# Rewriting the front of a hybrid transformer block: transposed q and k projections, both heads per scan, an LRU interleaved with attention, and an instruction order from a list schedule

## The chip, the cores and the metric

The kernel runs on one core of one Trainium2 chip. The time is the device time of one execution in microseconds (us). The engines are TensorE (PE, with its weight loads as PEld), VectorE (DVE), ScalarE (ACT), GpSimd (POOL) and SyncE (SP, which here only issues DMAs).

## The reference

One transformer block on 1024 tokens of width 1024, in fp32. A hybrid mixer stands in front, a squared-ReLU MLP behind:

```python
h = rms_norm(x, norm1_g)
proj = h @ w_in                                   # 1024 x 2560
q, k, v, xl, gl = split(proj)                     # five times 512 columns
q = rms_norm(q per head of 64, q_norm_g); k = rms_norm(k per head of 64, k_norm_g)
# stick-breaking attention, 8 heads, strictly causal
z = q @ k.T / 8
w = sigmoid(z) * prod over later keys of (1 - sigmoid(z))    # only keys before the query
attn = w @ v
# RG-LRU on 512 channels
u = causal_depthwise_conv(xl, width 4)
r, i = sigmoid(blockdiag(u, w_rg) + b_rg), sigmoid(blockdiag(u, w_ig) + b_ig)
a = exp(-8 * r * softplus(-lam));  hs[t] = a[t] * hs[t-1] + sqrt(1 - a[t]**2) * i[t] * u[t]
lru = hs * gelu(gl)
x = x + concat([attn, lru]) @ w_out
x = x + square(relu(rms_norm(x, norm2_g) @ w_up)) @ w_down
```

## The kernel before

**Arithmetic.** Nearly every fp32 operand of a product is split into a high part (rounded to the fp32r type) and a low part (the rest), and a product is three matmuls: low by high, high by low, high by high (`mm3`, lines 62 to 65). ACT makes the high part with a copy, DVE or POOL the low part with a subtraction (`lo_part`, line 60).

**Stages.** The front computes everything up to the mixer's output, which it writes channel by channel to `mix_d` in DRAM. Behind it stand the output projection (tiles `po`, fed by `wr_o`, the loads of `w_out`, and `mr`, the loads of `mix_d`) and the MLP with its own ring of loads and a fixed order of its own.

**The front** begins with x: 128-token tiles are loaded, transposed on PE (`ptx`), multiplied by the norm's gain and split into `hTh` and `hTl` (channels on partitions, 1024 tokens). The rows' 1/rms goes in later: `rstd1` multiplies what is projected. Head pairs are called p (0 to 3), each 128 columns of q, k and v.

- `in_proj(p, ..., tp)` projects q, k and v of one pair for 256 tokens, with tokens on partitions: per 128 tokens 24 matmuls of 384 columns into `pd`. DVE squares and sums q and k per head, `rsqrt_mean` finds 1/sqrt by three Newton steps on DVE (lines 84 to 89), DVE multiplies by it, POOL by the gains; then both are split and transposed on PE (`pq`, `pk`, `pl`) into `qT`, `kH`, `kL`. v stays with tokens on partitions (`vv`). In `qT` and `kH` the 128 rows hold the high and the low part of one head of 64, so that one matmul of 128 rows gives two of the three products and a second of 64 rows, with `kL`, the third.
- `attention(p, h, c, ...)` works on one head and two row blocks of 128 queries, r = 2c and 2c+1, over keys in pieces of up to 512. PE makes `z` (lines 405 and 406, and 408 for the mask on the diagonal block), ACT the two sigmoids (lines 410 and 411), DVE the product over later keys by a scan (line 415), POOL `w` times it (line 416). PE transposes w (`pw`, line 426), ACT and DVE split it (`wth`, `wtl`), PE multiplies with v (`av`, line 435), and DVE stores the head's rows through `ob`.
- The LRU's recurrence (`lru_tile`, lines 341 to 366) runs for all four blocks of 128 channels once the first pair is projected: projection `pxl`, convolution, two gates (`pg`, full fp32 matmuls), `Tanh`, a reciprocal on DVE (line 358), `Sqrt`, the scan. The result goes to `lru_d` in DRAM. `gate(c, ch)` later projects `pgl`, computes the gelu by a sigmoid, and multiplies.

**What sets the order.** `ORDER` lists attention units (A p h c), projections (I p tp), weight loads (O, W) and gates (G c ch); Tile's scheduler then moves instructions of neighbouring units past each other where its own model finds it useful, DMA issues on SP's queue among them.

Of the kernel before, what the change touches and what calls it, by code (L numbers as in the profile page):

```python
# [28 lines left out]
NG = 4  # L29
NW = 11  # L30

ORDER = (
# [3 lines left out]
).split()  # L38
EPS = 1e-6
NEG = -1e30  # L40
# [3 lines left out]
def kernel(ctx, tc, x, norm1_g, w_in, conv_w, conv_b, w_rg, b_rg, w_ig, b_ig,  # L44
# [13 lines left out]

# [7 lines left out]

    const = pool(ctx, "const")
    small = pool(ctx, "small", bufs=6)
    dram = pool(ctx, "dram", space=DRAM)
    ps_d = pool(ctx, "ps_d", bufs=2, space=PSUM)  # L70
# [8 lines left out]

    def rsqrt_mean(ssq, n, cols):  # L80
        v = small.tile([P, 8], F32, tag="rs_v", name="rs_v")[:, :cols]
        y = small.tile([P, 8], F32, tag="rs_y", name="rs_y")[:, :cols]
        m = small.tile([P, 8], F32, tag="rs_m", name="rs_m")[:, :cols]
# [9 lines left out]
    def transpose_pair(name, rows, gain, pools, dst_h, dst_l, col):  # L93
        for b in range(KC // 2):
            pt = bank(pools[b % len(pools)], [2, 2, P], f"pt{name}_{b}")
            for j in range(2):
                kc = 2 * b + j
                for i in range(2):
                    nc.tensor.transpose(pt[:, j, i, :], rows[i][:, kc * P:(kc + 1) * P], ident)
            for j in range(2):  # L100
                kc = 2 * b + j
                src = pt[:, j].rearrange("p i t -> p (i t)")
                oh = dst_h[:, kc, col:col + 2 * P]
                nc.scalar.mul(oh, src, gain[:, kc:kc + 1])
                nc.vector.scalar_tensor_tensor(dst_l[:, kc, col:col + 2 * P], src, gain[:, kc:kc + 1], oh.bitcast(F32),
                                               op0=ALU.mult, op1=ALU.subtract)

    nc.scalar.preload_act_table_set("sigmoid_and_others")
    ident = const.tile([P, P], F32, name="ident")
    make_identity(nc, ident)  # L110
    identr = const.tile([P, P], F32R, name="identr")
    identb = const.tile([P, P], BF16, name="identb")
    maskb = const.tile([P, P], BF16, name="maskb")

    mix_d = dram.tile([D, S], F32, name="mix_d")
    lru_d = dram.tile([AW, S], F32, name="lru_d")
    rs_d = dram.tile([NT, P], F32, name="rs_d")
    rs_row = rs_d.rearrange("t p -> (t p)").unsqueeze(0)
    rstd1 = const.tile([P, NT], F32, name="rstd1")
    gain1 = const.tile([P, NT], F32, name="gain1")  # L120
    rs2 = const.tile([P, NT], F32, name="rs2")

    left1 = ExitStack()
    hp = pool(left1, "hT")
    hTh = hp.tile([P, KC, S], F32R, name="hTh")
    hTl = hp.tile([P, KC, S], F32R, name="hTl")
    qkvE = pool(left1, "qkvE")
    wp = pool(left1, "wp", bufs=8)
    mp = pool(left1, "misc")


    def load_w(eng, name, src, n, wr=None):
        if wr is None:
            wr = wp.tile([P, 384], F32, tag="wr", name=f"wr_{name}", bufs=4)[:, :n]
        wh = wp.tile([P, 384], F32R, tag="wh", name=f"wh_{name}", bufs=8)[:, :n]
        wl = wp.tile([P, 384], F32R, tag="wl", name=f"wl_{name}", bufs=8)[:, :n]
        nc.sync.dma_start(wr if len(src.shape) == 2 else wr.rearrange("p (a b) -> p a b", a=src.shape[1]), src)
        nc.scalar.copy(wh, wr)
        lo_part(eng, wl, wr, wh)
        return wh, wl  # L140

    def load_pair(p, engs, raws=None):
        return [load_w(engs[kc % len(engs)], f"p{p}_{kc}",
                       w_in[kc * P:(kc + 1) * P, 0:3 * AW].rearrange("p (a b) -> p a b", a=3)[:, :, P * p:P * (p + 1)], 384,
                       raws[kc] if raws else None)
                for kc in range(KC)]

    XL0 = 3 * AW
    GL0 = XL0 + AW

    def load_cols(name, c0, engs):
        return [load_w(engs[kc % len(engs)], f"{name}_{kc}", w_in[kc * P:(kc + 1) * P, c0:c0 + 256], 256) for kc in range(KC)]

    def proj_cols(ws, j, ch, name):
        pd = bank(ps_d, [512], name)
        for kc in range(KC):
# [829 lines left out]
```

## Time and profile before

| | before |
|---|---|
| time, median of 3 runs | 1190.53 us (1189.09 to 1193.4) |
| span of the profiled execution | 1188.2 us |
| PE busy | 1140.8 us (96%) |
| DVE busy | 934.5 us (79%) |
| ACT busy | 603.7 us (51%) |
| POOL busy | 541.1 us (46%) |
| mean granted clock of PE | 0.983 |
| first matmul of the output projection | 459.0 us |

The profile is one execution. A stretch of the span has its own busy times, so the front (0 to 459 us) is read apart from what follows. The start of a matmul is recorded and its end is modelled: the distance between two starts in a stretch without waits says what one costs, its duration does not.

### The profile page before, as it was taken

To read this page: it belongs to the slowest core of one execution; us is meant where nothing else is said; L and a number is where in the kernel's file an instruction comes from. 1 tells how busy PE (TensorE), PEld (TensorE's weight loads), DVE (VectorE), ACT (ScalarE), POOL (GpSimd) and SP (SyncE) were. 2 spreads that over 40 slices of the span, in tenths; PEclk is the share of its full clock that TensorE was granted. 3 is DMA by queue.
4 is the path that set the end of the run, shared out by engine and by line. 5 is a ranking of instruction groups with operands and counts; after the bars stand their busy time and mean duration, and the time that the engine had idled before them with its cause. 6 is when DMAs were issued, how large, how long until landed. Compare 5 with 4: busy or idle time off the path is not lost.

```text
span 1188.2 us, 16104 instructions
## 1 busy us (share of the span) xinstructions
PE 1140.8 (96%) x5410; PEld 936.0 (79%) x5410; DVE 934.5 (79%) x1458; ACT 603.7 (51%) x1203; POOL 541.1 (46%) x506
## 2 busy tenths in 40 slices
PE   7999999999999968999999999999999999999998
PEld 7876777778888747888878888887887788888787
DVE  7789998899998887224776768998758667889975
ACT  7554665666665663136642584443456127743441
POOL 1357754664446683100244356762303444658331
PEclk9998999999999978999999999999999999999999
DMA  8110010410101284202344323554533333245654
GB/s 268 46 54 36 18 52 28 132 38 7 53 7 35 71 303 133 71 1 81 106 142 124 98 72 98 168 170 152 166 116 116 116 115 98 63 130 162 190 167 158
DMA packets 80787, 123.58 MB, mean 104 GB/s; under 512 B 10256, under 2 KB 28736, under 8 KB 80704
## 3 DMA queue, kind: packets, MB, share of 16 engines
q1 hardware_dynamic: 78400, 118.35, 32.0%
q10 hardware_dynamic: 2304, 4.20, 0.9%
q8 instruction: 43, 0.70, 0.3%
q14 instruction: 40, 0.33, 0.1%
HBM read 107.83 MB, written 14.68 MB: 103 GB/s over the span
## 4 chain that ended last, share of the span: by engine, by line
PE 70%; DVE 16%; issue 5%; DMA 3%; ACT 3%; POOL 2%; SPq 0%; DVEq 0%; ACTq 0%; POOLq 0%
PE p L577 24%; PE pa L577 11%; PE pb L577 5%; PE pc L577 4%; PE po L63 3%; PE po L64 3%; PE po L65 3%; DVE g L415 2%; PE av L435 2%; PE pd L63 2%; PE pd L64 2%; PE pd L65 2%; PE z L406 2%; PE pw L426 2%; POOL r_ea L577 1%
## 5 line engine op out<-in xcount | busy, mean ns | idle before, releaser
L416 POOL TENSOR_TENSOR w<-w,g 128x128 f32<-128x128 f32 (+3 forms) x96 | 101.4, 1064 | 102.7 <-DVE g L415 50.9
L415 DVE TENSOR_TENSOR_SCAN g<-g 128x128 f32<-128x128 f32 (+3 forms) x96 | 112.5, 1184 | 5.0 <-ACT g L410 4.1
L577 POOL TENSOR_TENSOR r_sb<-r_sb,r_sa 128x512 f32<-128x512 f32 x16 | 24.2, 1514 | 183.5 <-DMA r_sb<-in_w_up_dram 158.0
L577 DVE TENSOR_TENSOR U<-p,U 128x512 f32<-128x512 f32 x80 | 55.1, 688 | 63.0 <-PE p L577 62.7
L63 PE MATMUL pd<-wh_p,hTl 128*128 128x384 f32 x256 | 91.7, 359 | 9.5 <-DVE vv L180 4.4
L577 POOL TENSOR_TENSOR U<-U 128x512 f32<-128x512 f32 x48 | 69.4, 1452 | 68.8 <-ACT U L577 44.5
L577 PE MATMUL p<-m1t,st 128*128 128x512 f32 x384 | 91.2, 396 | 2.6 <-DVE U L577 2.6
L577 PE MATMUL p<-m0t,st 128*128 128x512 f32 x384 | 89.6, 391 | 1.3 <-DVE U L577 1.3
L64 PE MATMUL pd<-wl_p,hTh 128*128 128x384 f32 x256 | 90.2, 352 | 0.3 <-DVE wl_p L60 0.3
L577 PEld LDWEIGHTS p<-m1t,st 128*128 128x128 f32 x384 | 73.1, 191 | 19.4 <-issue 3.0
L65 PE MATMUL pd<-wh_p,hTh 128*128 128x384 f32 x256 | 87.9, 343 | 0.0
L577 PEld LDWEIGHTS p<-m0t,st 128*128 128x128 f32 x384 | 71.9, 188 | 17.7 <-ACT sb L577 1.7
L577 PE MATMUL p<-m0b,sb 128*128 128x512 f32 x288 | 68.0, 392 | 0.0
L577 PE MATMUL p<-m1b,sb 128*128 128x512 f32 x288 | 67.3, 391 | 0.0
L577 PEld LDWEIGHTS p<-m1b,sb 128*128 128x128 f32 x288 | 54.1, 188 | 11.8
L577 PEld LDWEIGHTS p<-m0b,sb 128*128 128x128 f32 x288 | 53.8, 188 | 11.5
L577 ACT ACTIVATE U<-U 128x512 f32<-128x512 f32 x96 | 58.9, 630 | 6.1 <-DVE U L577 3.1
L430 ACT CAST wth<-pw 128x512 fp32r<-128x512 f32 (+1 forms) x80 | 42.6, 547 | 37.5 <-PE pw L426 25.5
L410 ACT ACTIVATE g<-z 128x128 f32<-128x128 f32 (+3 forms) x96 | 48.1, 501 | 26.1 <-PE z L408 10.9
L63 PEld LDWEIGHTS pd<-wh_p,hTl 128*128 128x128 f32 x256 | 49.3, 193 | 13.2 <-DVE vv L180 5.3
L60 DVE TENSOR_TENSOR wtl<-pw,wth 128x512 fp32r<-128x512 f32 (+1 forms) x80 | 49.3, 628 | 9.9 <-ACT wth L430 9.5
L426 PE MATMUL pw<-ident,w 128*128 128x128 f32 x288 | 48.2, 285 | 5.4 <-DVE wtl L60 3.0
(302 smaller groups left out, 3218.8 us busy)
## 6 DMA issues: line engine op xcount, KB each, us to landing
wr_p<-in_w_in_dram SPq DMA_DIRECT2D x24, 192.0 KB, 2.7
xt<-in_x_dram SPq DMA_DIRECT2D x8, 512.0 KB, 7.5
wr_o<-in_w_out_dram SPq DMA_DIRECT2D x8, 512.0 KB, 3.8
mr<-mix_d SPq DMA_DIRECT2D x8, 512.0 KB, 6.8
x<-in_x_dram SPq DMA_DIRECT2D x16, 256.0 KB, 6.5
r_a<-in_w_up_dram SPq DMA_DIRECT2D x16, 256.0 KB, 2.7
r_b<-in_w_up_dram SPq DMA_DIRECT2D x16, 256.0 KB
r_sa<-in_w_up_dram SPq DMA_DIRECT2D x16, 256.0 KB
```

Of the source, the lines that this page charges most:

```text
L60: eng.tensor_tensor(lo, src, hi.bitcast(F32), op=ALU.subtract)
L63: nc.tensor.matmul(ps, al, bh, start=start, stop=False)
L64: nc.tensor.matmul(ps, ah, bl, start=False, stop=False)
L65: nc.tensor.matmul(ps, ah, bh, start=False, stop=stop)
L406: nc.tensor.matmul(z, qT[hs, h, qr], kL[hs, k0:k0 + kn], start=False, stop=not diag)
L410: nc.scalar.activation(g[:, :kn], z, AF.Sigmoid, scale=-1.0)
L415: nc.vector.tensor_tensor_scan(gr, gr, gr, g[:, kn:kn + 1], op0=ALU.mult, op1=ALU.bypass)
L416: nc.gpsimd.tensor_tensor(w[:, :kn], w[:, :kn], g[:, 1:kn + 1], op=ALU.mult)
L426: nc.tensor.transpose(pw[:, i * P:(i + 1) * P], wrow[rr][j // 4][:, j % 4 * P:(j % 4 + 1) * P], ident)
L430: nc.scalar.copy(wth[:, :nw], pw[:, :nw])
L435: nc.tensor.matmul(av[:, q0:256], vv[:, 2 * m + jj, h, :], wt[:, 256 * jj:256 * jj + 256 - q0], start=m == 0 and jj == 0 and wt is wtl, st ...
L577: ins = getattr(self.eng, op)(*args, **kw)
```

## The change

Everything of the front is written again; the output projection and the MLP stay, except that `rsqrt_mean` takes one power (-0.5) on POOL in place of the three Newton steps.

A new class `Plan` records each instruction with its engine, an assumed duration, and the tiles that it reads and writes. `record_front` records the units in the sequence of a new `ORDER`: C (constants), X (two token tiles of x), W (weights), R (the row of 1/rms), Q p ch (q and k of a pair for 512 tokens), V (v of two pairs for 512 tokens), L c ch (one LRU block of 128 channels for 512 tokens, with its gelu), A p c (attention of both heads of a pair for two row blocks). `schedule` is a list schedule: at each step the engine that can start earliest takes its ready instruction of the earliest unit; tiles have counted slots. The instructions are then issued in that order, each through `Pinned`, which keeps an engine's instructions in program order.

- **q and k** are projected with channels on partitions (24 matmuls of 512 columns each), so the transposes `pq`, `pk`, `pl` go. The sum of squares per head comes from four full fp32 matmuls with two moving columns (`ones2`), 1/sqrt from a power on POOL; the result is spread over 64 columns by ACT, transposed on PE (`rb`) and multiplied on DVE.
- **v** is projected for two pairs at once, 256 columns.
- **z**: for each row block and piece of keys, three products of 64 rows for each of the two heads, head 0 on partitions 0 to 63 and head 1 on 64 to 127, one after the other in turn, into the two halves of `z` (two banks). One burst holds two row blocks.
- **Sigmoids and scans** take both heads in one instruction: the scan of a diagonal piece runs over both heads' keys, with the constant row `K1` that restarts it at the second head. A piece that continues an earlier one keeps one scan per head.
- **LRU**: `Exp` and `Gelu_apprx_tanh` on ACT in place of the reciprocal and of the sigmoid form of gelu; per block the two `Sqrt`, two `Exp`, two `Gelu` are kept together. Nothing goes through `lru_d`; the row of 1/rms is made on PE in place of the detour through DRAM.

The core of the diff:

```diff
+ORDER = (
+    "C1 C0 X2 Wq0 X3 Wv0 R1 X1 Q01 X0 Wl0 Q00 V00 Wq1 R0 V01 A03 L00 A02 Wl1 L01 Q11 "
+    "Q10 A13 Wq2 L10 A10 L11 Q21 A12 Wv1 Wl2 A00 Q20 A11 V11 Wl3 V10 A22 A23 A01 L20 L21 L30 "
+    "Wq3 L31 A21 Q31 Q30 A20 A33 A32 A30 A31 "
+).split()
...
+    def chain(pd, key, col, ch, name):
...
+                    E.pe.matmul(pd[:], w[:, 1, s], E.hTh[:, kc, m], start=kc == 0, stop=False)
+                    E.pe.matmul(pd[:], w[:, 0, s], E.hTl[:, kc, m], start=False, stop=False)
+                    E.pe.matmul(pd[:], w[:, 0, s], E.hTh[:, kc, m], start=False, stop=kc == KC - 1)
...
+    def qunit(p, ch):
...
+            chain(pd, key, P * w, ch, f"p{'qk'[w]}{p}{ch}")
...
+                for t in range(4):
+                    E.pe.matmul(ps[:, 2 * t:2 * t + 2], sq[:, t * P:(t + 1) * P], E.ones2, start=True, stop=True)
...
+            op("POOL", 1637, lambda w=w: E.gps.tensor_tensor(sm[:, 8 * w:8 * w + 8], sm[:, 8 * w:8 * w + 8], E.mhalf[:, 0:8], op=ALU.pow),
...
+                    E.pe.transpose(rb[:, t * P:(t + 1) * P], sq[:, t * P:(t + 1) * P], E.ident)
...
+            op("DVE", 684, lambda f=f, rb=rb: E.dve.tensor_tensor(f[:], f[:], rb[:], op=ALU.mult), r=[f, rb], w=[f], what=f"nrm{p}{ch}")
...
+    def vunit(pp, ch):
...
+                        E.pe.matmul(pd[:, 0:256], E.hTh[:, kc, s], w[:, 1], start=kc == 0, stop=False)
...
+    def lunit(c, ch):
...
+            op("ACT", 620, lambda T=T: E.act.activation(T[:, 0:512], T[:, 0:512], AF.Sqrt), r=[T], w=[T], set="sqrt", grp=c, what=f"sqrt{nm}")
...
+            op("ACT", 620, lambda y=y: E.act.activation(y[:, 0:512], y[:, 0:512], AF.Gelu_apprx_tanh), r=[y], w=[y], set="gelu", grp=c, what=f"gelu{nm}")
...
+    def aunit(p, c):
...
+                    for n, (a, b) in enumerate(((1, 0), (0, 1), (0, 0))):
+                        for h in range(2):
+                            hs = slice(HD * h, HD * h + HD)
+                            E.pe.matmul(z[:, h, :kn], q[hs, a, cols], k[hs, b, :kn], start=n == 0, stop=n == 2 and not diag)
...
+                    if diag:
+                        gr = G[:, 0:2 * n - 1][:, ::-1]
+                        E.dve.tensor_tensor_scan(gr, gr, E.K1[:, 512 - kn:513 + kn][:, ::-1], 1.0, op0=ALU.mult, op1=ALU.add)
+                        return
...
+    plan = Maker()
+    record_front(plan, E, ORDER)
+    plan.schedule()
+    for o in plan.order:
+        o.fn()
+    front.close()
...
-        nc.vector.tensor_scalar(y.bitcast(I32), v.bitcast(I32), -0.5, float(0x5F3759DF), op0=ALU.mult, op1=ALU.add)
-        for _ in range(3):
-            nc.vector.scalar_tensor_tensor(m, y, -0.5, v, op0=ALU.mult, op1=ALU.mult)
-            nc.vector.tensor_tensor(m, m, y, op=ALU.mult)
-            nc.vector.scalar_tensor_tensor(y, m, 1.5, y, op0=ALU.add, op1=ALU.mult)
+        nc.gpsimd.tensor_tensor(y, v, E.mhalf[:, :cols], op=ALU.pow)
         return y
```

More of the change, by code (lines that the diff above doesn't have):

```diff
@@ new lines, with dve, dve2, act @@
+PTAGS = ("z", "pd", "pw", "av")
+MM = {512: 227, 384: 173, 256: 117, 128: 109}
+KEEP = {"PE": 0, "DVE": -77, "ACT": -95, "POOL": -40, "SP": 0}
+def dve(n):
+    return 210 + 0.93 * n
+def dve2(n):
+    return 230 + 1.45 * n
+def act(n):
+    return 185 + 0.82 * n
+def gps(n):
+    return 350 + 1.95 * n
+class V:
+    def __init__(self, plan, tag, name):
+        self.plan, self.tag, self.name = plan, tag, name
+        self.wr, self.rd, self.real = {}, {}, None
+        self.slot, self.ops, self.allocs = None, {}, []
+        if tag is not None:
+            plan.queue.setdefault(tag, []).append(self)
+    def get(self):
+        if self.real is None:
+            self.real = self.plan.make(self)
+        return self.real
+    def __getitem__(self, k):
+        return self.get()[k]
@@ new lines @@
+    E.pe, E.dve, E.act, E.gps, E.sp = (Pinned(e) for e in (nc.tensor, nc.vector, nc.scalar, nc.gpsimd, nc.sync))
+    E.vec = const.tile([P, 42], F32, name="vec")
+    E.mhalf = const.tile([P, 8], F32, name="mhalf")
+    nc.vector.memset(E.mhalf, -0.5)
+    gain2 = E.vec[:, 32:40]
+    front = ExitStack()
+    fc = pool(front, "fc", side="right")
+    hp = pool(front, "hT", side="right")
+    E.hTh = hp.tile([P, KC, S], F32R, name="hTh")
+    E.hTl = hp.tile([P, KC, S], F32R, name="hTl")
+    for nm, shape in (("rstd1", [NT]), ("var1", [NT]), ("epsv", [NT]), ("gain1", [NT]), ("gcol", [1]), ("t_a", [4]), ("t_b", [4]), ("t_c", [4]),
+                      ("sp_", [4]), ("nsp", [4]), ("ones2", [2]), ("bd", [2, NCT, P]), ("rsb", [S]), ("K1", [1025])):
+        setattr(E, nm, fc.tile([P] + shape, F32, name=nm))
@@ new lines @@
+    E.identb = fc.tile([P, P], BF16, name="identb")
+    E.maskb = fc.tile([P, P], BF16, name="maskb")
+    nc.vector.tensor_copy(E.identb, ident)
+    nc.gpsimd.memset(E.maskb, 0.0)
+    nc.gpsimd.affine_select(out=E.maskb, in_=E.maskb, compare_op=ALU.is_gt, fill=NEG, base=0, pattern=[[-1, P]], channel_multiplier=1)
+    nc.vector.memset(E.ones2, 0.0)
+    for h in range(2):
+        nc.vector.memset(E.ones2[HD * h:HD * h + HD, h:h + 1], 1.0)
+    nc.vector.memset(E.K1, 0.0)
+    nc.vector.memset(E.K1[:, 512:513], 1.0)
@@ new lines, with make @@
+    spools = {t: pool(front, f"f_{t}", space=PSUM if t in PTAGS else None, side=("right" if t in ("w", "wr", "v", "lg", "f", "qk") else None) if t not in PTAGS else None)
+              for t in COUNT}
+    class Maker(Plan):
+        def make(self, v):
+            shape, dt = SHAPE[v.tag]
+            return spools[v.tag].tile([P] + shape, dt, tag=f"{v.tag}{v.slot}", name=v.name)
+    plan = Maker()
[3 more added lines that the diff above has]
+        o.fn()
@@ L90, in rsqrt_mean @@
-        return y
[L93 to L140, printed above, removed]
@@ L494 @@
-    right1.close()
-    left1.close()
+        nc.gpsimd.tensor_tensor(y, v, E.mhalf[:, :cols], op=ALU.pow)
+        return y
     xp1 = pool(ctx, "x1")
```

854 lines of the change are left out of this document (541 added, 313 removed), and 3 rows, old and new, of the table ORDER.

## Prediction

> **What bounds the kernel now.** I read the 40 slices of the page first, which show TensorE (PE) busy nearly everywhere, and then cut the span where the first matmul of the output projection starts, at 459.0 us. The busy times by stretch:
>
> ```profile
> core 0: us, PE busy (x) PEld busy (x) DVE busy (x) ACT busy (x) POOL busy (x), PEclk, DMA share, GB/s
> 0.00:459.00 459.00, 423.45 (x2275) 351.01 (x2275) 407.43 (x773) 277.55 (x630) 242.66 (x316) 0.96 0.24 76
> 459.00:1188.20 729.20, 717.36 (x3136) 584.98 (x3136) 527.07 (x686) 326.15 (x574) 298.48 (x190) 0.99 0.39 122
> ...
> 10.00:420.00 410.00, 392.73 (x2139) 327.36 (x2137) 372.88 (x727) 247.25 (x574) 217.99 (x290) 0.98 0.19 58
> 420.00:459.00 39.00, 25.54 (x118) 19.48 (x118) 31.63 (x37) 23.91 (x45) 22.58 (x18) 0.76 0.62 217
> 459.00:480.00 21.00, 21.00 (x82) 17.06 (x83) 15.81 (x12) 4.64 (x5) 11.47 (x5) 0.88 0.68 224
> ```
>
> The second row is the part behind the front: 729 us, PE busy for 717 of them at a clock of 0.99. The change leaves that part alone but for a few small operations (below), so I carry it over as 729 us. All of the forecast is about the first row. There PE is busy for 423 of 459 us, but VectorE (DVE) for 407 too: two engines are close to full, and the waits of PE say which one holds the other up. The longest waits of PE in the front:
>
> ```profile
> PE av L435 <- DVE wtl L60: 5.8, 2, 5.0
> PE ptx L99 <- DMA xt<-in_x_dram: 4.5, 1, 4.5
> ```
>
> Apart from the first load of x, it is DVE that PE waits for. But a busy PE is not a PE at its peak, since the ends of matmuls are modelled. So I price PE work by the distance between starts, in stretches where nothing waits (columns: start, duration, engine, line, operation, tiles, shape):
>
> ```profile
> 29.26 0.33 PE L63 MATMUL pd<-wh_p,hTl 128*128 128x384 f32 x1
> 29.43 0.33 PE L64 MATMUL pd<-wl_p,hTh 128*128 128x384 f32 x1
> ...
> 93.89 1.02 PE L351 MATMUL pg11r<-u,bd_r 128*128 128x512 f32 x2
> 94.74 1.02 PE L351 MATMUL pg11i<-u,bd_i 128*128 128x512 f32 x2
> ...
> 407.20 0.27 PE L405 MATMUL z<-kH,qT 128*128 128x128 f32 x1
> 407.41 0.32 PE L406 MATMUL z<-kL,qT 64*128 64x128 f32 x1
> 407.66 0.23 PE L408 MATMUL z<-maskb,identb 128*128 128x128 bf16 x1
> 407.70 0.47 PE L64 MATMUL pgl<-hTl,wh_gl 128*128 128x512 f32 x1
> ...
> 408.24 0.40 PE L63 MATMUL pgl<-hTh,wl_gl 128*128 128x512 f32 x1
> 408.48 0.40 PE L64 MATMUL pgl<-hTl,wh_gl 128*128 128x512 f32 x1
> ...
> 411.68 0.28 PE L435 MATMUL av<-wtl,vv 128*128 128x256 f32 x1
> 411.80 0.28 PE L435 MATMUL av<-wth,vv 128*128 128x256 f32 x1
> ...
> 412.56 0.95 PE L426 MATMUL pw<-ident,w 128*128 128x128 f32 x7
> 413.27 0.48 PE L405 MATMUL z<-kH,qT 128*128 128x512 f32 x1
> 413.67 0.50 PE L406 MATMUL z<-kL,qT 64*128 64x512 f32 x1
> 414.10 0.39 PE L405 MATMUL z<-kH,qT 128*128 128x256 f32 x1
> 414.42 0.38 PE L406 MATMUL z<-kL,qT 64*128 64x256 f32 x1
> 414.73 0.23 PE L408 MATMUL z<-maskb,identb 128*128 128x128 bf16 x1
> ```
>
> So a split matmul of 512 columns costs 0.23 us, one of 384 columns 0.17, one of 256 columns 0.12, a transpose 0.10 (seven in 0.71), a full fp32 matmul of 512 columns 0.85 in two passes. The surprise is z: 0.40 and 0.43 at 512 columns, 0.32 and 0.31 at 256, 0.21 and 0.25 at 128. The pair alternates between a form of 128 rows (kH) and one of 64 rows (kL), and every change of form costs some 0.2 us on top of the 0.23.
>
> The front's PE work from that: q, k, v 768 x 0.17 = 132; xl and gl 384 x 0.23 = 88; transposes of x and of the weights w 352 x 0.10 = 36; transposes of q, k and k's low part 160 x 0.10 = 16; av 256 x 0.12 and 64 x 0.10 = 37; gates 16 x 0.85 = 14; z 48 x 0.83 + 16 x 0.74 (384 columns, put between its neighbours) + 16 x 0.63 + 16 x 0.46 + 64 masks x 0.04 = 72. Sum 395 us. Of the 459 us, 64 are therefore lost. Some 20 go in 420 to 459, where PE is busy for 25.5 us at a clock of 0.76, worth 19. Some 5 go at the start (the 4.5 us wait). The other 39 go between 10 and 420: 17 idle (410 less 392.7), 8 by the clock of 0.98, the rest at the seams between groups.
>
> **The change, PE.** q and k transposed: 4 pairs x 2 chunks x 2 x 24 = 384 matmuls x 0.23 = 88; v for two pairs at a time: 384 x 0.12 = 46; against the 132 of before that is nothing. xl and gl stay at 88, the 352 transposes at 36, av at 37, gates at 14. The 160 transposes of q and k go (-16); 64 that carry 1/rms into columns and 8 for the rows' scale come (+7). New are 64 sums of squares, a full fp32 matmul with two moving columns: two passes each. No row shows such a one. Below lies half a transpose a pass (64 x 2 x 0.05 = 6), above the gates' 0.85 each (54). I take a transpose's 0.10 a pass, 13 us, since a transpose too loads 128 columns of weights and streams little.
>
> z is the largest term. It becomes 48 steps of six matmuls of 64 rows, heads 0 and 1 alternating between partitions 0 to 63 and 64 to 127, in 24 bursts, so the form changes twice a burst. If the two heads' matmuls run side by side, a step costs three distances: 24 x 3 x 0.23 + 8 x 3 x (0.17 + 0.12 + 0.10) = 26, with 48 changes x 0.2 and the masks 38. If they run one after the other, 52 + 12 = 64. If going from one half to the other costs as much as the change of form does in the rows above, 144 x 0.43 + 48 x (0.37 + 0.32 + 0.23) + 3 = 109. No row shows two halves at work at once. I take 38: the excess in the rows sits on a change of form, and stays away where the form stays; inside a burst it stays, and the two heads share neither rows of the array nor an output bank.
>
> By the Trainium skill, TensorEngine Tiling (Array Packing), Key Properties, "Different tiles can execute LdWeights and Matmul in parallel", while a change of the tiling mode drains the engine; by that rule z is the 38 that I took. The trace agrees with the second half (0.40 to 0.43 for 0.23); the first half no run here shows yet.
>
> PE's sum after: 88 + 46 + 88 + 36 + 7 + 37 + 14 + 13 + 38 = 367, **28 less** than before; with z's and the sums' other ends, 360 to 479.
>
> **The other engines.** Does one of them take over? The first two rows are DVE's busy time from 0 to 459 on what touches rs_y and sq, the others groups by line and shape (count, busy us, mean ns):
>
> ```profile
> 0.00:459.00 459.00, 58.86 (x220) 0.96 0.24 76
> 0.00:459.00 459.00, 26.26 (x32) 0.96 0.24 76
> ...
> L358 DVE RECIPROCAL ext<-ext 128x512 f32<-128x512 f32 x8 | 26.7, 3341 | 1.1 <-POOL ext L356 1.0
> L60 DVE TENSOR_TENSOR wtl<-pw,wth 128x512 fp32r<-128x512 f32 x48 | 32.5, 684 | 7.7 <-ACT wth L430 7.4
> L348 DVE SCALAR_TENSOR_TENSOR u<-ext,vec,u 128x512 f32<-128x512 f32 x24 | 23.9, 1018 | 2.6 <-ACT u L346 2.4
> L104 ACT ACTIVATE hTh<-ptx,gain 128x256 fp32r<-128x256 f32 x32 | 13.5, 494 | 0.3 <-PE ptx L99 0.3
> L359 ACT ACT_TABLE_LOAD x4 | 5.1, 1283 | 0.1
> ```
>
> DVE loses the Newton steps and the scaling by them (58.9), the squares and their sums (26.3) and the reciprocals (26.7), 112 us. It gains 16 products with the 1/rms tile at 0.68 and 8 joined multiply-adds at 1.02, with small ones some 25. 407 - 112 + 25 = 320 at the most, for other things shrink too: the scan of a diagonal block covers both heads in one instruction. ScalarE (ACT) gains, for q and k, four passes of 512 columns x 16, at about twice the 0.494 of a 256-column one at the most (63 us), and has 16 table loads for 8, +10: 278 + 73 = 351 if nothing of the old q, k path is taken off, and that path goes. GpSimd gains 16 low parts and 16 powers of eight numbers. No row shows a power; between nothing and a reciprocal's 3.3 us each it is 0 to 53, hidden behind other projections either way, and it loses the same kind of low parts elsewhere. All stay under PE's 367. So PE remains the bound, now with no second engine beside it.
>
> **What is lost beside the sum.** Middle: the 17 us of idle wait for a DVE that is 89% full; at 320 of some 425 us it is 75% full, and I leave 4 of the 17. The clock's 8 and the seams stay. Start: what x needs before the first product.
>
> ```profile
> 0.74 0.40 SPq L222 DMA_DIRECT2D xt<-in_x_dram  x1
> ...
> 7.49 0.33 SPq L273 DMA_DIRECT2D vrow<-in_conv_w_dram  x1
> ```
>
> Before, x went out first and the ten small loads later. Now C1's ten small loads stand first on SP's queue, 0.33 us each, 3 us; and the first product needs 512 tokens transposed (16 pieces of 0.494 on ACT) where 256 did (8), 4 us. I take +6, since the weights' casts fill part. End: again attention alone, four units of pair 3, paced by scans; I leave the 20. Handover to the output projection:
>
> ```profile
> 413.25 0.43 SPq L889 DMA_DIRECT2D wr_o<-in_w_out_dram  x1
> ...
> 457.19 0.45 SPq L443 DMA_DIRECT2D mix_d<-ob  x1
> ...
> wr_o<-in_w_out_dram SPq DMA_DIRECT2D x8, 512.0 KB, 3.8
> mr<-mix_d SPq DMA_DIRECT2D x8, 512.0 KB, 6.8
> ```
>
> Before, the first load of w_out was issued 44 us ahead of the last store of attention, past it on SP's queue. Now every instruction of the front is held in its order. If the loads must queue behind the last store, 6.8 us of landing and the casts are open; if they pass, nothing. I take +3, with 0 to 10 as its ends. Behind the front, the four Newton chains on the norm of h become one power on GpSimd, which is idle there (298 of 729 us): nothing either way, and if that cover were gone, a few of at most 3.3 us.
>
> Losses: 64 + 6 - 13 + 3 = 60. The front then ends at 367 + 60 = 427, 32 us earlier; the span is 1188.2 - 32 = 1156. The median of before, 1190.53, lies 2.3 us over its profiled span, so the forecast is **1158.5 us**.
>
> **Rivals.** (1) Better than that: the fixed order fills the middle and half of the end, losses of 30 in place of 60: 1128. For it speaks that only PE is full; against it, that 64 were lost before. (2) The heads run one after the other: +26, 1184. (3) The sums of squares cost the gates' price: +41, 1199. (4) **The order holds PE up:** each q or k chunk goes through eight steps on four engines (square, sum, power, spread, transpose, product, two halves) and PE's next instruction in the fixed order waits at the queue's head, with all matmuls behind it; or the handover pays its 10. Twice the middle's old idle, +17: 1176. (5) **Slower:** going from one half of the array to the other costs what the change of form costs; z is 109, +71: 1229. It decides from 32 us over 288 matmuls, 0.11 us each above the shared price. Only the 0.2 us of the z rows speaks for it. That the change does not do what it says would show as (4), with the old waits in new places.
>
> **How the numbers follow.** Forecast 0.40, (1) 0.20, (2) 0.10, (3) 0.04, (4) 0.17, (5) 0.09. The range reaches from below (1) to (3): 1118 to 1200; outside lie (5) and the far end of (1). What a measurement of this kernel can tell from no change is about 0.5%, 6 us. Faster: forecast, (1), (4), half of (2): 0.82. Same: the rest of (2) and part of (3): 0.08. Slower: 0.10.
>
> **What would show it.** Right: the first output projection near 427 us; two z matmuls of one step starting within 0.1 us of each other; DVE near 300 us in the front; no wait of PE above 5 us between 20 and 400. Wrong: z starts 0.23 or 0.43 apart all along a burst; the sums of squares over 0.3 us apart; PE waiting for GpSimd's power or for ACT behind table loads; or more than 5 us between the last av and the first po. The forecast falls altogether if the part behind the front does not keep its 729 us.

## The result and the profile after

The changed kernel takes 1198.53 us (median of 5 runs, 1197.89 to 1202.43) against 1189.09 of the kernel before (5 runs, 1184.65 to 1193.4): a ratio of 1.0091, 95% interval 1.0066 to 1.0117. It is slower by 0.9%, where 1158.5 us, 2.6% faster, was forecast. The time lies inside the range, on the side that had a chance of 0.10. The profiled execution has a span of 1199.3 us (1188.2 before).

The view of busy times by stretch, for the changed kernel, cut near the first attention product (`z`, at 59.1 us), near the last projection (375.8), and at the last matmul of the output projection (`po`, 571.0):

```profile
core 0: us, PE busy (x) PEld busy (x) DVE busy (x) ACT busy (x) POOL busy (x), PEclk, DMA share, GB/s
0.00:60.00 60.00, 43.43 (x220) 36.05 (x222) 27.38 (x91) 36.52 (x81) 20.59 (x34) 0.91 0.36 115
60.00:376.00 316.00, 309.95 (x1896) 258.79 (x1893) 194.20 (x256) 197.90 (x343) 168.01 (x176) 0.99 0.12 38
376.00:571.00 195.00, 154.06 (x726) 124.66 (x725) 81.88 (x102) 74.40 (x126) 54.68 (x44) 0.80 0.22 75
```

The middle is what the forecast hoped for and more: PE is busy for 310 of 316 us at a clock of 0.99, and DVE for only 194. The third row is where the time went: 195 us in which PE is busy for 154 and gets 0.80 of its clock. The longest waits of PE say by whom it is held there:

```profile
PE av L708 <- DVE wt L708: 25.4, 16, 3.0
PE rb L708 <- ACT sq L708: 9.1, 4, 5.1
...
PE po L697 <- POOL mix0l L694: 4.5, 1, 4.5
PE po L697 <- DVE mix0l L694: 4.2, 1, 4.2
```

`wt` is the tile with the high and low parts of the transposed weights; the product with v (`av`) waits for it. All but two of its 16 waits, and all but 1.5 us of their sum, lie behind 376. Near the end of attention the timeline shows one turn after another (start, duration, engine, line, operation, tiles):

```profile
477.95 1.23 PE L708 MATMUL av<-wt,v 128*128 128x256 f32 x4 [1.40 <-DVE wt L708]
...
478.97 1.05 PE L708 MATMUL pw<-ident,w 128*128 128x128 f32 x4
...
480.06 0.59 ACT L708 CAST wt<-pw 128x512 fp32r<-128x512 f32 x1 [0.48 <-PE pw L708]
480.68 0.69 DVE L708 TENSOR_TENSOR wt<-pw,wt 128x512 fp32r<-128x512 f32 x1 [0.65 <-ACT wt L708]
...
481.43 1.22 PE L708 MATMUL av<-wt,v 128*128 128x256 f32 x4 [1.40 <-DVE wt L708]
...
482.45 0.63 PE L697 MATMUL po<-wo,mix0l 128*128 128x512 f32 x1
```

Four transposes fill the bank `pw`, ACT casts it into `wt`, DVE makes the low part, PE multiplies: 3.48 us from one av to the next, one step after the other (of the 21 such distances behind the last projection the middle one is 3.62). The plan's slots (`COUNT`) hold one `pw` and one `wt`. The kernel before has two of each (`bufs=2` in its lines 72, 428 and 429), and in its timeline the transposes of the next group begin while ACT still casts this one:

```profile
450.71 0.59 ACT L430 CAST wth<-pw 128x512 fp32r<-128x512 f32 x1 [1.39 <-PE pw L426]
...
450.93 0.63 PE L426 MATMUL pw<-ident,w 128*128 128x128 f32 x4
...
451.33 0.69 DVE L60 TENSOR_TENSOR wtl<-pw,wth 128x512 fp32r<-128x512 f32 x1 [1.42 <-ACT wth L430]
451.71 0.59 ACT L430 CAST wth<-pw 128x512 fp32r<-128x512 f32 x1
```

In the changed kernel, as long as projections stand beside, the turn hides behind them; behind the last projection it is all that there is. The tile views of `av`, before and after, from the last projection on (count, duration min/median/max, first and last start):

```profile
L435 PE MATMUL av<-wtl,vv x32: 221/386/583, 416.2 to 456.0; 128*128 128x256 f32 x27, 128*128 128x128 f32 x5
L435 PE MATMUL av<-wth,vv x32: 275/319/416, 416.3 to 456.0; 128*128 128x256 f32 x27, 128*128 128x128 f32 x5
```

```profile
L708 PE MATMUL av<-wt,v x88: 222/415/582, 395.4 to 482.2; 128*128 128x256 f32 x68, 128*128 128x128 f32 x20
```

Before, 64 matmuls of av, 16 groups of four, were left behind the last projection and took 40 us, 2.5 us a group; the first came 0.2 us behind that projection. Now there are 88, 22 groups, the first of them comes 19.5 us behind the last projection, and they take 87 us, 3.9 us a group.

In the timeline of its first burst z shows that the two heads do run side by side: twelve matmuls, six a head, half of them of 384 and half of 512 columns, in 1.43 us up to the mask. One head after the other they would take 2.4 us at the distances of the prediction.

```profile
59.10 1.50 PE L708 MATMUL z<-k,q 64*128 64x384 f32 x12
60.53 0.40 PE L708 MATMUL z<-maskb,identb 128*128 128x128 bf16 x4
```

**The balance.** I price every matmul of the changed kernel by the distances of the prediction, z's changes of form included, and call lost what is left of a stretch:

| stretch | lost, forecast | lost, measured |
|---|---|---|
| start, to 60 us | 5 + 6 = 11 | 25.1 |
| 60 us to the last projection (375.8) | 39 - 13 = 26 | 15.5 |
| end and handover, with the output projection, to the last po (571.0) | 20 + 3, and the 8 that po lost before (94.9 us for 384 x 0.227) = 31 | 76.5 |

The matmuls of the front are those that the prediction counted, so at its prices they come to its 367 again; the part from the last po to the end takes 628.3 us where it took 634.4. So of the 43 us between the forecast span (1156) and the measured one, 14 come at the start, some 45 behind the last projection, and some 16 go the other way: 10 in the middle, 6 in the part behind.

### The profile page after: what moved, and what is told of

It is laid out like the page before. It is cut to its first block, busy times and chain, and to the rows that moved or that the text cites. A ratio compares the mean times of both kernels' runs of the same rounds, so it can differ in the third digit from the quotient of the medians.

```text
span 1199.3 us, 15521 instructions
## 1 busy us (share of the span) xinstructions
PE 1123.8 (94%) x5546; PEld 926.4 (77%) x5546; DVE 792.2 (66%) x1055; ACT 607.1 (51%) x1072; POOL 526.0 (44%) x439
## 4 chain that ended last, share of the span: by engine, by line
PE 71%; DVE 10%; ACT 6%; issue 5%; POOL 5%; DMA 2%; SPq 0%; ACTq 0%; POOLq 0%; DVEq 0%
PE p L859 24%; PE pa L859 9%; PE pq L708 6%; PE pc L859 4%; PE pv L708 4%; PE av L708 3%; PE pgl L708 3%; PE z L708 2%; PE pw L708 2%; PE po L697 2%; PE po L699 2%; PE po L698 2%; PE pb L859 2%; POOL r_ea L859 2%; PE pxl L708 2%
## 5 line engine op out<-in xcount | busy, mean ns | idle before, releaser
L708 POOL TENSOR_TENSOR w<-w,G 128x1024 f32<-128x1024 f32 (+3 forms) x48 | 78.0, 1637 | 57.0 <-ACT w L708 34.1
L708 PE MATMUL pq<-hTh,wq 128*128 128x512 f32 x256 | 89.5, 409 | 1.9 <-ACT rsb L708 1.9
L708 PE MATMUL av<-wt,v 128*128 128x256 f32 (+1 forms) x320 | 60.4, 316 | 26.0 <-DVE wt L708 25.4
L708 DVE TENSOR_TENSOR wt<-pw,wt 128x512 fp32r<-128x512 f32 (+1 forms) x80 | 50.4, 629 | 50.9 <-ACT wt L708 50.2
L708 PEld LDWEIGHTS av<-wt,v 128*128 128x128 f32 x320 | 51.1, 212 | 41.9 <-DVE wt L708 36.2
L859 POOL TENSOR_TENSOR r_sb<-r_sb,r_sa 128x512 f32<-128x512 f32 x16 | 21.5, 1342 | 107.7 <-DMA r_sb<-in_w_up_dram 65.7
L708 ACT CAST wt<-pw 128x512 fp32r<-128x512 f32 (+1 forms) x80 | 43.4, 543 | 42.2 <-PE pw L708 39.8
L859 ACT ACTIVATE U<-U 128x512 f32<-128x512 f32 x96 | 58.9, 629 | 6.4 <-DVE U L859 3.4
L708 DVE TENSOR_TENSOR_SCAN G<-G,K 128x769 f32<-128x769 f32 (+3 forms) x32 | 54.8, 1723 | 9.7 <-ACT G L708 8.8
L708 PEld LDWEIGHTS pq<-hTh,wq 128*128 128x128 f32 x256 | 48.7, 190 | 12.4 <-ACT rsb L708 2.6
L708 ACT ACTIVATE G<-z 128x1024 f32<-128x1024 f32 (+3 forms) x48 | 38.3, 816 | 26.7 <-PE z L708 16.3
```

What stands on the lines that cost most here:

```text
L708: return tc.keep_in_program_order(getattr(self.eng, op)(*args, **kw))
L859: ins = getattr(self.eng, op)(*args, **kw)
```

## The experiments

The theory behind them: the attention that is left alone goes single file through the one `pw` and the one `wt`, and at half the clock. The rivals: the scans on DVE set its pace, as the prediction had it; the pairing of the heads or the front's PE sum is not what it seems. All times are medians. The kernel before stood at 1188.6 to 1190.1 in the four groups of runs, so ratios are to it. The last two columns are from the one profiled execution of each run, which can lie some us off the median (e1's took 1183.48, e4's 1195.58). Where a run changes what the plan counts (e1, e2, e3, e5, e6 and what builds on them) or the units' sequence, the list schedule can come out in another order; e7, e9, e13 and e14 leave the plan as it was in the changed kernel.

| run | us | ratio, 95% interval | last av | last po |
|---|---|---|---|---|
| changed kernel | 1198.53 | 1.0091 [1.0066, 1.0117] | 482.2 | 571.0 |
| e1_banks | 1176.33 | 0.9893 [0.9856, 0.9929] | 445.4 | 548.7 |
| e2_warm | 1190.31 | 1.0003 [0.9988, 1.0018] | 474.7 | 564.8 |
| e3_hilo | 1193.39 | 1.0022 [1.0009, 1.0035] | 474.8 | 563.5 |
| e4_start | 1199.83 | 1.0075 [1.0052, 1.0098] | 478.4 | 567.6 |
| e5_pw | 1192.25 | 1.0032 [1.0012, 1.0052] | 473.5 | 561.7 |
| e6_wt | 1201.90 | 1.0106 [1.0075, 1.0137] | 472.0 | 573.0 |
| e7_noscan | 1193.47 | 1.0033 [1.0011, 1.0054] | 476.9 | 566.7 |
| e8_combo | 1170.37 | 0.9837 [0.9801, 0.9873] | 438.1 | 541.5 |
| e9_zserial | 1199.37 | 1.0078 [1.0054, 1.0103] | 482.4 | 571.3 |
| e10_warm | 1166.95 | 0.9808 [0.9780, 0.9835] | 436.1 | 538.7 |
| e11_noscan2 | 1166.84 | 0.9797 [0.9769, 0.9824] | 433.3 | 536.6 |
| e12_order | 1169.10 | 0.9818 [0.9792, 0.9844] | 437.3 | 538.8 |
| e13_zburst | 1214.19 | 1.0211 [1.0192, 1.0230] | 494.5 | 583.1 |
| e14_zbreak | 1235.17 | 1.0388 [1.0359, 1.0417] | 512.8 | 601.5 |
| e15_chain | 1173.31 | 0.9870 [0.9853, 0.9886] | 443.6 | 547.0 |

### The single buffers: e1_banks, e5_pw, e6_wt

Pair 3 comes last, when the banks of the projections (`pd`) and the tiles of older q and k (`qk`) fall free. e1 lets its groups use two of them in turn with the old one, three in all; e5 has the first line alone, e6 the second.

```diff
-                pw = plan.tile("pw", f"pw{p}{c}{m}{h}")
+                late = p == 3
+                pw = plan.tile(("pw", "pd", "pd")[nlate[0] % 3] if late else "pw", f"pw{p}{c}{m}{h}")
...
-                ww = plan.tile("wt", f"wt{p}{c}{m}{h}")
+                ww = plan.tile(("wt", "qk", "qk")[nlate[0] % 3] if late else "wt", f"wt{p}{c}{m}{h}")
```

> Pair 3's 20 groups of attention (transpose, cast, low part, av) take their bank and their split tile in turn from one of three (the old one and two that the projections have done with) in place of one. If the end is slow because each group waits for the one bank and the one tile of the group before it, starts of av come some 2 us apart in place of 3.5, the last av moves from 481 to about 460 us and the span falls by 15 us or more. If DVE's queue (scans ahead of low parts) or the halved clock sets the pace, the groups stay over 3 us apart and the span moves by under 5 us.

> Only the PSUM bank of the transposed weights is taken in turn from three banks for pair 3; the SBUF tile of their high and low parts stays single. Theory (the groups of attention are held by a chain through both single buffers: transposes, cast, low part, av, which freeing both cut by 22 us): with the transposes out of the chain, cast 0.59, low part 0.69 and av about 1.1 with their hand-overs remain, some 2.6 us a group in place of 3.5 in 20 groups, so a gap near 2.6 and about 10 us below the changed kernel, 1188. Rival (this bank alone is what holds them): a gap near 1.0 and the whole 22 us, 1176. Rival (the tile alone holds them): gap 3.5, 1198.

> Only the SBUF tile of the weights' high and low parts is taken in turn from three tiles for pair 3; the PSUM bank of the transposes stays single. Theory (chain through both): transposes 0.5 to 1.05, cast 0.59 and low part 0.69 still follow each other through the one bank, some 2.3 us a group, so a gap of 2.3 to 2.7 and about 10 us below the changed kernel, 1188. Rival (this tile alone holds them): gap near 1.0, 1176. Rival (the bank alone): gap 3.5, 1198.

Measured: both together 22 us below the changed kernel, and faster than the kernel before by 1.1%. The bank alone is worth 6, the tile alone nothing that can be told. The tile view of `av` in e1, e5 and e6, in this order:

```profile
L711 PE MATMUL av<-wt,v x88: 221/308/582, 395.8 to 445.4; 128*128 128x256 f32 x68, 128*128 128x128 f32 x20
```

```profile
L711 PE MATMUL av<-wt,v x88: 221/358/583, 395.0 to 473.5; 128*128 128x256 f32 x68, 128*128 128x128 f32 x20
```

```profile
L711 PE MATMUL av<-wt,v x88: 221/415/584, 395.7 to 472.0; 128*128 128x256 f32 x68, 128*128 128x128 f32 x20
```

The same 88 matmuls take 50, 78 and 76 us in place of 87; with both buffers freed a group takes 2.3 us, no more than in the kernel before. Neither bank nor tile alone gives the 22 us, as its rival had it: freeing one leaves the other's turn. In e5 the timeline shows what is left of it:

```profile
419.45 1.22 PE L711 MATMUL av<-wt,v 128*128 128x256 f32 x4 [1.53 <-DVE wt L711]
...
420.71 0.58 ACT L711 CAST wt<-pw 128x512 fp32r<-128x512 f32 x1 [3.02 <-PE av L711]
...
421.33 0.69 DVE L711 TENSOR_TENSOR wt<-pw,wt 128x512 fp32r<-128x512 f32 x1 [1.93 <-ACT wt L711]
...
422.07 1.22 PE L711 MATMUL av<-wt,v 128*128 128x256 f32 x4 [0.55 <-DVE wt L711]
```

The cast starts when the last av has read `wt`, so a turn is 2.62 us here: av, cast, low part, as the theory had it. Over the 22 groups the middle distance is 3.30, so the theory's 10 us were too many. In e6 it is 3.48, where 2.3 to 2.7 was expected: with the bank single the turn hardly shrinks. And e6 shows a second thing: its av ends 10 us earlier, but its first po comes at 478.8 (450.7 in the changed kernel, where 54 po matmuls already stand among the av), so the work only changed places. The same holds for e1: of the 37 us that its av ends earlier, 22 reach the last po.

### The clock: e2_warm, e10_warm

e2 gives every group of pair 3 in the changed kernel four pairs of matmuls whose output nobody reads, in free `pd` banks. e10 puts three into the group's own `pw` ahead of the transposes, on top of e8 (below).

```diff
+                    for i in range(4):
+                        dm = plan.tile("pd", f"dm{p}{c}{m}{h}{i}")
+                        def warm(dm=dm):
+                            for n in range(2):
+                                E.pe.matmul(dm[:], E.hTh[:, 0, 0:P], E.hTh[:, 0, 0:512], start=n == 0, stop=n == 1)
+                        op("PE", 2 * 227, warm, w=[dm], what="warm")
```

```diff
# e10
+                if late:
+                    def warm(pw=pw):
+                        for n in range(3):
+                            E.pe.matmul(pw[:], E.hTh[:, 0, 0:P], E.hTh[:, 0, 0:512], start=n == 0, stop=n == 2)
+                    op("PE", 3 * 227, warm, w=[pw], what="warm")
```

> Beside each of pair 3's 20 groups, four pairs of matmuls of 512 columns, whose output nobody reads, fill PE where it stood idle. If the halved clock is what makes the end long, the clock reads 1.0 from 376 to 480 us, transposes and av of a group take half as long, some 1.2 us less for each of 20 groups, and the span falls by 15 to 24 us. If the pace is set off PE, the span stays within 4 us, or is longer by what the added matmuls hold up.

> The combination, with three 512-column matmuls whose output is overwritten unread put into the bank of the transposed weights ahead of each group of transposes of pair 3: 20 x 0.68 us. Theory (the half clock costs in the tail beside the buffers): the clock rises from 0.60 to 0.83 in 380 to 440 to 0.9 or more, the last av comes 4 to 8 us earlier than at 438, the time is 1163 to 1167. Rival (with the buffers free TensorE has no room in the tail; what is added holds the groups up): the last av stays or comes later, 1170 to 1178.

Two stretches of 20 us in the changed kernel, then the same two in e2:

```profile
400.00:420.00 20.00, 12.93 (x64) 10.03 (x64) 12.80 (x14) 8.30 (x14) 5.89 (x8) 0.57 0.02 8
420.00:440.00 20.00, 12.65 (x68) 10.49 (x70) 11.25 (x15) 8.78 (x16) 6.14 (x12) 0.65 0.02 7
```

```profile
400.00:420.00 20.00, 19.90 (x121) 16.30 (x121) 15.22 (x17) 8.98 (x16) 5.90 (x8) 1.00 0.02 7
420.00:440.00 20.00, 20.00 (x131) 16.86 (x129) 11.56 (x15) 9.97 (x17) 6.08 (x12) 1.00 0.12 38
```

The sixth number behind the duration is the clock. In e2 PE has more to do and gets all of its clock, and the time falls by 8 us although some 36 us of work (160 matmuls x 0.227, an estimate) came in. So the half clock was a cost of its own, beside the buffers, though half of the least expected, 15 us. With the buffers freed it is worth less: from 380 to 440 us the clock is 0.74 in e8 and 0.87 in e10, and e10 stands 3 us below e8 by the medians, but the intervals of the two overlap; in the traces its last po comes 2.8 us earlier.

By the Trainium skill, TensorE: Matmul & The Clock Gate, Part 1, PE is granted either half or all of its clock while one core works, according to how busy it was in a window of about 3.4 us. The trace agrees in the two values: in the changed kernel the clock is 0.50 from 382 to 398 us and 1.00 from 399 to 402, and the 0.57 above is a mean of both. How busy PE must be for all of it, no run here shows.

### The scans: e7_noscan, e11_noscan2

The prediction held that attention alone is paced by the scans. Both runs leave pair 3's scans out, e7 in the changed kernel, e11 in e8.

```diff
                     if diag:
+                        if p == 3:
+                            E.dve.tensor_copy(G[:, kn:n], G[:, kn:n])
+                            return
...
-                    for h in range(2):
+                    for h in range(2 * (p < 3)):
```

> Pair 3's scans are left out (a copy of one column stands in their place, so the break weights of pair 3 are not multiplied up); the buffers and the rest stay. The scans take 26 us of VectorE in the 80 us from 380 to 460. Theory (the single buffers hold the groups; the scans only now and then delay a low part): the median gap stays at 3 us or more, the last av comes 3 to 10 us earlier, and the time is about 5 us below the changed kernel, 1193. Rival (the tail is paced by the scans, as the prediction put it): the last av comes at 460 or before, the gap falls under 2.5, and the time is 18 us or more below, 1180 or less.

> The combination, with pair 3's scans left out as before (a copy of one column stands in their place). Theory (with the single buffers gone the scans of VectorE are the next thing in the tail's way): the last av comes 10 us or more before 438, the time is 1160 or less, twice or more what leaving them out was worth in the changed kernel (5). Rival (the tail is then held by the chain of q and k's last rows before it and by the clock): 3 to 5 us, 1165 to 1168.

Measured: 5 us and 3.5 us, the latter with overlapping intervals. In e7 the turn is nearly as long as before. From its timeline:

```profile
422.84 1.22 PE L711 MATMUL av<-wt,v 128*128 128x256 f32 x4 [1.40 <-DVE wt L711]
...
426.32 1.22 PE L711 MATMUL av<-wt,v 128*128 128x256 f32 x4 [1.40 <-DVE wt L711]
```

Again 3.48 us, with no scan on DVE anywhere near. The scans do not set the pace in the changed kernel. With the buffers freed they do keep groups apart (the middle distance is 1.50 us in e8 and 0.96 in e11), but the last av comes only 4.8 us earlier, where 10 or more was expected: the expectation that they would be the next thing in the way (e11) was wrong.

### The start: e3_hilo, e4_start

In e3 the two pieces of x that share one PSUM bank are both copied by ACT before DVE makes the two low parts. e4 moves the ten small loads behind the first loads of x and weights.

```diff
-                op("DVE", 474, lw, r=[(z, j), gain1, (hT, ("h", kc, tp))], w=[(hT, ("l", kc, tp))], what=f"hTl{tp}")
+                late.append((lw, j, kc))
+                if j % 2:
+                    for lw, jj, k in late:
+                        op("DVE", 474, lw, r=[(z, jj), gain1, (hT, ("h", k, tp)), (hT, ("h", kc, tp))], w=[(hT, ("l", k, tp))], what=f"hTl{tp}")
+                    late.clear()
```

```diff
-    "C1 C0 X2 Wq0 X3 Wv0 R1 X1 Q01 X0 Wl0 Q00 V00 Wq1 R0 V01 A03 L00 A02 Wl1 L01 Q11 "
+    "C0 X2 Wq0 X3 C1 Wv0 R1 X1 Q01 X0 Wl0 Q00 V00 Wq1 R0 V01 A03 L00 A02 Wl1 L01 Q11 "
```

> Of each bank of transposed x, ACT now makes both high parts before DVE makes both low parts. If ACT and DVE taking turns on one bank is what makes the start long, ACT's waits for hTl (8.4 us before 60 us) go, the first z comes at some 51 to 53 us in place of 59, and the span falls by 5 to 8 us. If the loads of x and of the weights set the start, the first z stays within 2 us of 59 and the span within 2.

> The unit with the ten small loads (C1) moves behind X2, Wq0 and X3 in the sequence. If these loads on SP's queue are what delays the start, as the prediction had it, the first transpose of x comes at about 5 us in place of 8.1, the first z 3 us earlier, and the span falls by 3 us. If the start is paced by ACT and DVE, the first transpose comes earlier and the first z does not move by more than 1 us.

ACT's longest wait in the first 60 us, changed kernel and e3:

```profile
ACT hTh L708 <- DVE hTl L708: 8.4, 15, 0.6
```

```profile
ACT hTh L713 <- DVE hTl L713: 4.0, 7, 0.6
```

Half the turns between the two engines, 5.8 us earlier at the first z (53.3 for 59.1), 5 us in the time. The first z lies between 52.9 and 53.3 in the six traces that have this change, and between 58.9 and 60.5 in the others but e4. In e4 the first transpose of x comes at 4.9 for 8.1, the first z at 56.7 and the last po 3.4 us earlier, but the median shows nothing of it; whether the small loads cost the time something stays open.

### The pairing of heads: e9_zserial, e13_zburst, e14_zbreak

The changed kernel issues head 0 and head 1 in turn. e9 issues a step's three passes of head 0, then its three of head 1; e13 all passes of a burst by head; e14 keeps e9's order and puts a matmul over all 128 rows between the heads.

```diff
# e9
-                    for n, (a, b) in enumerate(((1, 0), (0, 1), (0, 0))):
-                        for h in range(2):
+                    for h in range(2):
+                        for n, (a, b) in enumerate(((1, 0), (0, 1), (0, 0))):
# e13
-                for (r, k0, kn, diag) in steps:
+                for h, (r, k0, kn, diag) in [(h, s) for h in range(2) for s in steps]:
# e14, on e9
+                        if h:
+                            E.pe.matmul(z[:, h, kn - P:kn], E.identb, E.maskb, start=True, stop=True)
```

> The changed kernel, with each step's three z passes of head 0 issued first and then the three of head 1, in place of the heads' passes pair by pair; the same matmuls. Theory (the pairs run beside each other on the two halves of the rows, and TensorE bounds the stretch from 60 to 376): the z work goes from about 38 us to between 51 and 64, hardly hidden before 376, so the time is 11 to 24 us above the changed kernel, 1210 to 1222. Rival (the pairing is worth nothing, since other engines set the pace there): within 4 us of it, 1195 to 1203.

> The changed kernel, with all passes of head 0 of a burst (up to two steps, six passes) issued first, then all of head 1. Theory (each half of the rows takes its matmuls from a queue of its own, several deep): the pairs still start within 0.02 us of each other and the time is that of the changed kernel, 1196 to 1203. Rival (only some three matmuls are looked ahead): part of the passes run alone, 0.23 us each, and the time is 5 to 24 us above it.

> The changed kernel, with a 128-row matmul of 128 columns (its output is overwritten unread) between head 0's three passes and head 1's three in each of the 48 steps, so that they can't run beside each other. Theory (pairing makes 38 us of 64, and TensorE bounds 60 to 376): 26 us of passes and 48 times 0.06 to 0.3 for the matmul between and its changes of form, three quarters of it ahead of 376: 20 to 35 us above the changed kernel, 1218 to 1234. Rival (TensorE has room there): less than 10 above, under 1208.

e9 did not test what it was made for: its time is the same, and its first burst takes the same 1.43 us (first row below), though the passes are issued three by three. e13 breaks part of the pairing: 1.89 us from z to mask (second row).

```profile
60.23 1.50 PE L708 MATMUL z<-k,q 64*128 64x384 f32 x12
61.66 0.40 PE L708 MATMUL z<-maskb,identb 128*128 128x128 bf16 x4
```

```profile
59.32 1.96 PE L708 MATMUL z<-k,q 64*128 64x384 f32 x12
61.21 0.40 PE L708 MATMUL z<-maskb,identb 128*128 128x128 bf16 x4
```

The groups of z with 512 columns, changed kernel, e13 and e14 (busy us, mean ns):

```profile
L708 PE MATMUL z<-k,q 64*128 64x512 f32 x144 | 22.7, 441 | 0.1
```

```profile
L708 PE MATMUL z<-k,q 64*128 64x512 f32 x144 | 32.6, 450 | 0.2 <-ACT w L708 0.2
```

```profile
L710 PE MATMUL z<-k,q 64*128 64x512 f32 x144 | 45.3, 490 | 0.0
```

In e14 their busy time doubles, and the time rises by 37 us, a little over its forecast. But e14 breaks the pairing only within a step: in the records of single matmuls of the first burst, the second head of the first step starts 10 ns beside the first head of the second step. So half the pairing is left, and the matmul between with its changes of form must make more of the rise than the forecast had; the two were not separated. By the Trainium skill, TensorEngine Tiling (Array Packing), Key Properties, tiles work in parallel and a change of mode drains the engine; the trace now agrees with the first half as well: in the changed kernel the two matmuls of a pair start 3 ns apart in the median. The two runs tell more: ahead of the last projection the bursts of z take 7.6 us more in e13 and 21.9 in e14, and the last projection, at 375.8 in the changed kernel, moves by 7.3 us to 383.1 and by 18.1 to 393.9. What is added to PE there shows nearly in full, so PE does bound that stretch.

### Combinations: e8_combo, e12_order, e15_chain

e8 is e1 with e3. e12 and e15 only change the order of the units, e12 on e8, e15 on e10:

```diff
# e12
-    "C1 C0 X2 Wq0 X3 Wv0 R1 X1 Q01 X0 Wl0 Q00 V00 Wq1 R0 V01 A03 L00 A02 Wl1 L01 Q11 "
-    "Q10 A13 Wq2 L10 A10 L11 Q21 A12 Wv1 Wl2 A00 Q20 A11 V11 Wl3 V10 A22 A23 A01 L20 L21 L30 "
-    "Wq3 L31 A21 Q31 Q30 A20 A33 A32 A30 A31 "
+    "C1 C0 X2 Wq0 X3 Wv0 R1 X1 Wl0 Q01 X0 Q00 V00 R0 V01 Wq1 A03 L00 Wl1 A02 L01 Q11 Q10 A13 "
+    "Wq2 L10 A10 L11 Q21 A12 Wv1 Wl2 A00 Q20 A11 V11 Wl3 V10 A22 A23 A01 L20 L21 L30 Wq3 L31 "
+    "A21 Q31 Q30 A20 A33 A30 A32 A31 "
# e15
-    "Wq3 L31 A21 Q31 Q30 A20 A33 A32 A30 A31 "
+    "Wq3 L31 Q31 Q30 A21 A20 A33 A32 A30 A31 "
```

> The banks and tiles in turn for pair 3 together with both copies to the high parts ahead of both low parts at the start. Alone they were worth 22 and 5 us against the changed kernel. Theory (they lie in different stretches, after 376 and before 60): they add, 1171, a ratio to the kernel before of 0.985. Rival (the earlier attention only waits longer in the tail for what follows): 1176, no more than the banks alone.

> The combination with the units recorded in another order (pair 3's query blocks 3, 0, 2, 1 in place of 3, 2, 0, 1; the loads of the second weights and the first rows of x and v moved by one or two places), which the kernel's own plan puts 3.3 us shorter. Theory (the plan ranks orders rightly where no buffer holds): 2 to 4 us less, 1167. Rival (the plan misses what decides in the tail): within 2 us or above, 1169 to 1176.

> The combination with the clock held (e10), with the last rows of q and k (Q31, Q30) recorded ahead of A21, so that attention of pair 2 lies beside their chain of normalisation. Theory (TensorE waits there for want of other work): 2 to 8 us below e10's 1167, 1159 to 1165. Rival (as the kernel's own plan has it, which puts it 4 us later, since pair 2's attention and the slots it holds are then late): 1167 to 1172.

e8 adds up, 28 us below the changed kernel. e12 cannot be told from e8. e15 went the rival's way, 6 us above e10: the first av comes 12.4 us behind the last projection (18.7 in e10), but PE is hardly fuller there (15.7 of the 24 us from 368, against 15.2), and attention then ends later, with 104 matmuls of av behind the last projection in place of 88.

```profile
L721 PE MATMUL av<-wt,v x104: 221/282/583, 379.8 to 443.6; 128*128 128x256 f32 x80, 128*128 128x128 f32 x24
```

The lowest median of the kernels that compute everything is that of e10, 1.9% faster than the kernel before (interval 1.6 to 2.2%); e8 and e12 cannot be told from it. Its longest waits of PE behind 368 show what remains:

```profile
PE po L710 <- DVE mix0l L707: 8.4, 1, 8.4
PE av L721 <- DVE wt L721: 6.3, 5, 3.0
PE rb L721 <- ACT sq L721: 5.9, 1, 5.9
```

## Why the prediction was wrong

**PE's work: right.** The counts of matmuls are met, so what could fail were the two prices that no row of before showed. From the first z of a burst to the matmul behind its masks, the 24 bursts take 40 us for the 38 taken, 25 of them in the 17 bursts ahead of the last projection. The sums of squares stand at 0.10 us a pass (eight start at 62.64, the next matmul at 63.45), which was the value taken. Rivals (2), (3) and (5) fall: heads one after the other, the gates' price, a price for going from one half of the array to the other. With (3) falls what set the upper end of the range: that the measured time lies inside it is luck.

**"So PE remains the bound, now with no second engine beside it": right up to 376, and there it led astray.** DVE is busy for 275 us up to the last av (482), under the 320 allowed, and the longest wait of PE between 20 and 376 is 1.9 us. But sums of busy time compare engines that work beside each other. Behind the last projection no engine is full (third row of the first fence): it is a chain over three engines, and its length is what counts. No sum shows that.

**The step that failed: "End: again attention alone, four units of pair 3, paced by scans; I leave the 20".** Four things in it were wrong. "Again": the kernel before had two banks and two tiles for the transposed weights, the changed one has one of each, so the end is not the old one. The mechanism: not the scans (5 us when left out) but these two single buffers, 22 us when pair 3 alone gets two more of each; what paced the end of the kernel before, no run tests. The amount: 88 matmuls of av are left, 64 were before, and the 19.5 us from the last projection to the first av, 0.2 before, have no term at all. And the cost of the half clock was carried over with the 20 though it grows with the stretch, 8 us by e2.

The diff shows `wt=1` and `pw=1` in `COUNT`. An estimate from rows of the profile before would have warned: four transposes at 0.10, a cast at 0.59, a low part at 0.68 and four av at 0.12 make 2.2 us a turn, some 48 us for the 22 groups when nothing overlaps, and 22 x 3.48 = 77 with the turn as it came out at half the clock, of the 87 measured. Of the tail's 45 us, the runs account for some 22 by the buffers, up to 8 by the clock and up to 5 by the scans; the three were not found to add, since with the buffers freed the last two shrink to some 3 each. From the last projection to the last po the changed kernel takes 195.2 us and e10, with buffers and clock mended, 170.7: some 21 us remain. The six groups more and the chain of the last q and k rows ahead of the first av lie in them, and the handover; what each of these would give was not isolated, and e15 shows that putting pair 2's attention beside the chain, in that one order, gains nothing.

**Handover: mis-sized, within its ends.** 3 us was taken, with 10 as the far end; PE waits 4.5 and 4.2 us for `mix0l`, some 9. The shorter wait stands in the middle of the attention, ahead of the first po at 450.7.

**Start: mis-sized.** 6 more was taken, 14 more than that were lost. One cause was not seen: ACT and DVE take turns on each bank of transposed x. Removing half of these turns gave 5 us; the rest stays open.

**Middle: better than forecast.** 15.5 us lost for 26, with PE busy for 310 of 316 us.

**Rival (4)** was nearest: the order holds PE up. It named the chain of q and k, whose waits sum to 9.1 us, and the handover; its price of 17 was too small and its place wrong, since the hold-up came where nothing else was left.

**The part behind** did not keep its 729 us but gave 6 us back: 628 us from the last po where it took 634, with the same number of matmuls:

```profile
571.00:1199.00 628.00, 616.40 (x2710) 506.94 (x2709) 488.79 (x606) 298.27 (x522) 282.76 (x185) 1.00 0.42 132
```

```profile
554.00:1188.00 634.00, 622.36 (x2710) 506.74 (x2708) 491.19 (x616) 298.51 (x522) 283.37 (x184) 1.00 0.42 131
```

Nothing in these rows says why. In the fifteen other traces, whose part behind is the same code, it takes 625.5 to 632.9 us, so some of the 6 may be scatter between executions; it stays open.

## What to carry to other kernels

When a reordering takes work out of a bound engine, look for the stretch that has nothing left beside it, compare its buffers with those of the kernel before, count its groups, and multiply by the longest turn through a single buffer, over all engines that the turn passes. Free such buffers together before judging one: here one alone gave 6 us and the other none, both gave 22. The second buffer need not cost space: here it was one that another stage had stopped using by then.

## What the runs showed of the hardware

- Matmuls of 64 rows on the other half of the array overtake those that wait for the first half: with three passes of one head issued ahead of three of the other, the records of single matmuls still show the pairs starting 10 ns apart in the median (3 ns when issued in turn) and the first burst takes the same 1.43 us. With six ahead it no longer does so throughout: in the first burst the second head's first matmul starts with the third of the first head, and the burst takes 1.89 us.
- Added work that nobody reads can shorten the time: some 36 us of matmuls brought the clock of 400 to 420 us from 0.57 to 1.00 and the end 8 us nearer.
- The power -0.5 of 128 x 8 elements on GpSimd takes 2.02 us, nearly as long as a product of 128 x 1024 there (2.09):

```profile
L708 POOL TENSOR_TENSOR w<-w,G 128x1024 f32<-128x1024 f32 x24 | 50.0, 2086 | 31.0 <-ACT w L708 22.0 <-issue 7.8 <-DVE qv L708 1.2
...
L708 POOL TENSOR_TENSOR qv<-qv,mhalf 128x8 f32<-128x8 f32 x16 | 32.3, 2021 | 13.5 <-DVE qv L708 13.5
```
